# RWKV-7 chains in a hybrid block: small passes moved from VectorE to ScalarE, joint reciprocal roots, and the substitution's rows spread by a transfer to DRAM and back

## The chip, the cores and the metric

The kernel runs on one core of one Trainium2 chip. The metric is the device time of an execution in microseconds (us); less is better. Engines are named as in the profile: PE is TensorE (PEld its weight loads), DVE is VectorE, ACT is ScalarE, POOL is GpSimd, SP is SyncE. SP, ACT and POOL can issue DMA transfers; all transfers share 16 DMA engines.

## The reference

One layer of an encoder block over 256 tokens of width 2048, all in float32. The input is normed and projected; the columns feed an RWKV-7 time mixer (16 heads of 64), a latent attention (8 heads) and two gates. The gated sum is projected and normed back in, then come a gated MLP with a causal convolution, and an embedding branch. The change touches only the RWKV-7 mixer:

```python
def step(state, inp):
    r_t, w_t, k_t, v_t, kk_t, a_t = inp
    sa = jnp.einsum('bhvk,bhk->bhv', state, -kk_t)
    state = (state * w_t[:, :, None, :]
             + sa[..., None] * (kk_t * a_t)[:, :, None, :]
             + v_t[..., None] * k_t[:, :, None, :])
    y_t = jnp.einsum('bhvk,bhk->bhv', state, r_t)
    return state, y_t
...
kk = heads(k * k_k)
kk = kk / jnp.maximum(jnp.sqrt(jnp.sum(kk * kk, axis=-1, keepdims=True)), 1e-12)
k = k * (1 + (a - 1) * k_a)
y = rwkv7_scan(r_h, heads(decay), k_h, v_h, kk, a_h)
mean = jnp.mean(y, axis=-1, keepdims=True)
var = jnp.mean(jnp.square(y - mean), axis=-1, keepdims=True)
y = ((y - mean) * lax.rsqrt(var + RW_GN_EPS)).reshape(B, S, RW_WIDTH)
```

## The kernel before

**The work in the large.** PE runs dense matmuls for nearly the whole span. Each weight chunk (128 x 1024 float32, 512 KB) is loaded by SP into one of three `raw` buffers; ACT casts each half to float32r (`hi`, line 148, five buffers) and DVE subtracts to get the rest (`lo`, line 149, five buffers). Three products (hi x hi, hi x lo, lo x hi; lines 183 to 185) give nearly float32 accuracy. A `raw` buffer is free again when its two `lo` are made, a `hi` or `lo` buffer when PE has used it.

**The RWKV chains.** Between some 187 and 590 us the eight pairs of heads run through `rw_pair`, woven into the dense matmuls of the projections, the attention branch and the gates. A pair is two heads on 128 partitions; two pairs (`par` 0 and 1) run in step as a duo; the four duos are called duo 0 to duo 3. A pair goes through these stages, each a few steps of the generator:

- Preparation: decay, key norm (`pq`, the root in `nv`), the key factor (line 792), the scaled keys and receptances `bk` and `kr`.
- `pg` (line 818): all Gram blocks on PE; DVE masks them (`gm`, line 821), ACT copies the strictly lower part (`n`, 823).
- Substitution: each 64 x 64 unit triangular block is inverted from its 16 x 16 diagonal blocks up. DVE gathers these blocks of both pairs (`dg`, 842) and subtracts them from the identity (848: the diagonal step). Then every partition of a group of 16 needs all 15 rows of its group: 15 stream shuffles (line 854) copy row i of each group to its 16 partitions in `rp16`. Then come 15 columns, each a product `pd` (861) and a reduction into `xc` (862), each dependent on the one before. Both pairs are done in these operations at once.
- The blocks are joined on PE: transposes `Y` (888), then `ph`, `px`, `ph`, `px` (line 882) with DVE between.
- Four chunks of 64 tokens in sequence, three steps each: `pc` (940), the copy `R` of two halves (941 on ACT, 942 on DVE), `pc` again (944), `av` of two halves (945 ACT, 946 DVE), `pc` (953), the state `sv` (955, DVE), which the next chunk's matmul (940) needs.
- Tail: output `yc` (964), group norm of `y` (970 to 982), `pm` (988, transpose-like matmuls of the normed `y`), gate, `yrw`.

**What sets the order.** `rw_pair` is a generator; each `yield` gives a number of dense units (one unit is six matmuls of 256 columns) that are put into the program before the next step: STEP is 2.4, CHUNK 2.8, SUB 1.56. The loop at the end of the stage advances the tail of the old duo, the current one, and the preparation of the next, in that order. What a step emits is then placed on each engine by the framework's list scheduler. Every engine takes its instructions strictly in program order, so an instruction that waits holds up all behind it on its engine.

## Time and profile before

| | |
|---|---|
| median of 3 runs | 1561.18 us (1561.16 to 1561.9) |
| the profiled execution | 1560.39 us, of which the span of its instructions is 1558.6 us |
| PE busy | 1538.0 us, 99% |
| DVE busy | 1182.2 us, 76% |
| ACT busy | 942.1 us, 60% |
| POOL busy | 60.9 us, 4% |
| granted PE clock | 0.997 |

How to read it: in a list of groups each row gives line, engine, operation, output<-inputs, shapes and count, then busy us and the mean ns of one, then the idle time of the engine before them and what ended it. In the list of waits stand the total, the number and the longest. In a row of windows stand the stretch, its length, then busy us and instructions of PE, PEld, DVE, ACT and POOL, the granted clock, the DMA share and GB/s. A timeline row starts with start and duration; the brackets hold the idle time before it. A row of DMA issues gives the size and the median us from issue to landing. Matmuls overlap, so the mean ns of one is longer than its share of the time.

### The profile page before, as it was taken

The page shows a single profiled execution, that of the slowest core. Times are in us where ns is not written, and L with a number is a line of the kernel's source. Part 1 is how long each engine was busy: PE and PEld are TensorE (multiplying, and loading weights), DVE is VectorE, ACT ScalarE, POOL GpSimd, SP SyncE. Part 2 cuts the span into 40 slices and gives each one's busy share as a digit, 9 for nine tenths or more (in the row PEclk, how much of TensorE's full clock was granted, in tenths as well). Part 3 has the DMA queues.
Part 4 walks back from the last instruction along what each step waited for, and adds up shares of the span by engine and source line. Part 5 has one row for each costly group of instructions (what it writes and reads, how often), then busy time and mean ns, then how long its engine had stood idle before and what let it go on. Part 6 is the DMA issues. An engine that isn't in the chain of part 4 may idle for free.

```text
span 1558.6 us, 29636 instructions
## 1 busy us (share of the span) xinstructions
PE 1538.0 (99%) x10850; PEld 1388.3 (89%) x10850; DVE 1182.2 (76%) x2670; ACT 942.1 (60%) x1944; POOL 60.9 (4%) x125
## 2 busy tenths in 40 slices
PE   9999999999999999999999999999999999999997
PEld 9989999999999999887888888888888888888886
DVE  7896687898989776557787777777777655777866
ACT  7686756566565555456766555555655555776653
POOL 0000201101011102000000000000000000000000
PEclk9999999999999999999999999999999999999998
DMA  8654555454444546865656555565655666666564
GB/s 304 192 172 141 154 173 164 138 171 129 147 150 136 160 153 200 306 199 167 203 174 205 198 181 202 179 203 179 206 181 190 175 192 195 197 197 191 166 200 148
DMA packets 80482, 285.19 MB, mean 183 GB/s; under 512 B 9040, under 2 KB 10320, under 8 KB 80336
## 3 DMA queue, kind: packets, MB, share of 16 engines
q1 hardware_dynamic: 77760, 279.48, 56.3%
q10 hardware_dynamic: 2576, 3.81, 0.7%
q8 instruction: 85, 1.39, 0.4%
q14 instruction: 61, 0.50, 0.1%
HBM read 281.16 MB, written 2.10 MB: 182 GB/s over the span
## 4 chain that ended last, share of the span: by engine, by line
PE 89%; DVE 6%; ACT 2%; DMA 1%; issue 1%; DVEq 0%; ACTq 0%
PE d L170 21%; PE d L174 11%; PE d L183 9%; PE d L185 8%; PE d L184 8%; PE o L196 7%; PE o L198 6%; PE o L200 6%; PE e L196 2%; PE e L198 2%; PE e L200 2%; DVE lo L149 2%; ACT hi L148 1%; DMA raw<-in_w_in 1%; PE tr L237 0%
## 5 line engine op out<-in xcount | busy, mean ns | idle before, releaser
L149 DVE TENSOR_TENSOR lo<-raw,hi 128x512 fp32r<-128x512 f32 x684 | 461.0, 690 | 213.9 <-ACT hi L148 208.5
L148 ACT CAST hi<-raw 128x512 fp32r<-128x512 f32 x684 | 410.7, 619 | 297.9 <-PE o L200 97.9
L183 PE MATMUL d<-uT,hi 128*128 128x256 f32 x1072 | 307.7, 287 | 0.7 <-ACT hi L161 0.6
L170 PE MATMUL d<-u,highs 128*128 128x512 f32 x1312 | 305.5, 390 | 0.0
L185 PE MATMUL d<-uT,lo 128*128 128x256 f32 x1072 | 300.5, 280 | 0.7 <-DVE lo L162 0.2
L184 PE MATMUL d<-uT,hi 128*128 128x256 f32 x1072 | 299.6, 279 | 0.1
L170 PEld LDWEIGHTS d<-u,highs 128*128 128x128 f32 x1312 | 243.3, 188 | 48.9
L148 ACT CAST highs<-raw 128x512 fp32r<-128x512 f32 x328 | 186.8, 616 | 115.0 <-DMA raw<-in_w_up 80.3
L183 PEld LDWEIGHTS d<-uT,hi 128*128 128x128 f32 x1072 | 201.7, 188 | 2.8 <-ACT hi L161 0.8
L185 PEld LDWEIGHTS d<-uT,lo 128*128 128x128 f32 x1072 | 201.5, 188 | 2.1 <-DVE lo L149 1.1
L184 PEld LDWEIGHTS d<-uT,hi 128*128 128x128 f32 x1072 | 201.7, 188 | 0.4 <-DVE uT L290 0.3
L149 DVE TENSOR_TENSOR hi<-raw,highs 128x512 fp32r<-128x512 f32 x164 | 112.7, 688 | 76.8 <-PE d L174 58.8
L174 PE MATMUL d<-u,lo 128*128 128x256 f32 x752 | 117.7, 280 | 0.0
L149 DVE TENSOR_TENSOR lo<-raw,highs 128x512 fp32r<-128x512 f32 x164 | 112.0, 684 | 0.0
L174 PE MATMUL d<-u,hi 128*128 128x256 f32 x656 | 103.3, 279 | 0.0
L174 PEld LDWEIGHTS d<-u,lo 128*128 128x128 f32 x752 | 101.7, 188 | 0.8
L174 PEld LDWEIGHTS d<-u,hi 128*128 128x128 f32 x656 | 91.5, 188 | 3.5
L198 PE MATMUL o<-lo,fsplit 128*128 128x512 f32 x264 | 88.6, 389 | 0.0
L196 PE MATMUL o<-hi,fsplit 128*128 128x512 f32 x264 | 88.5, 389 | 0.0
L200 PE MATMUL o<-hi,fsplit 128*128 128x512 f32 x264 | 88.4, 389 | 0.0
L1228 ACT ACTIVATE cy<-d 128x512 f32<-128x512 f32 x44 | 26.2, 597 | 67.8 <-PE d L174 67.8
L198 PEld LDWEIGHTS o<-lo,fsplit 128*128 128x128 f32 x264 | 49.6, 188 | 10.7 <-DVE lo L149 0.3
(389 smaller groups left out, 2550.9 us busy)
## 6 DMA issues: line engine op xcount, KB each, us to landing
raw<-in_w_up SPq DMA_DIRECT2D x176, 512.0 KB, 4.3
raw<-in_w_in SPq DMA_DIRECT2D x133, 512.0 KB, 3.6
raw<-in_w_down SPq DMA_DIRECT2D x88, 512.0 KB, 4.3
raw<-in_w_out SPq DMA_DIRECT2D x32, 512.0 KB, 4.4
raw<-in_w_pg SPq DMA_DIRECT2D x32, 512.0 KB, 3.6
raw<-in_w_bm SPq DMA_DIRECT2D x16, 512.0 KB, 3.7
raw<-in_w_br SPq DMA_DIRECT2D x16, 512.0 KB, 3.7
raw<-in_w_kv SPq DMA_DIRECT2D x8, 512.0 KB, 3.6
```

The costliest lines, as they stand in the source:

```text
L148: nc.scalar.copy(hi[:], raw[:, c:c + 512])
L149: tt(out=lo[:], in0=raw[:, c:c + 512], in1=hi[:].bitcast(F32), op=ALU.subtract)
L170: mm(ps[:, c, :], hi(i, col, P), mov[i][2], start=first and x == 0 and i == 0, stop=False)
L174: mm(ps[:, c, 0:T], lo(i, col, P), mov[i][0], start=False, stop=last and x == len(parts) - 1 and i == len(mov) - 1)
L183: mm(ps[:, c, :], hi(i, col, P), mov[i][:, 0:T], start=f, stop=False)
L184: mm(ps[:, c, :], hi(i, col, P), mov[i][:, T:2 * T], start=False, stop=False)
L185: mm(ps[:, c, :], lo(i, col, P), mov[i][:, 0:T], start=False, stop=l)
L196: mm(b[:], h, hi(i, g * 512, 512), start=f, stop=False)
L198: mm(b[:], h, lo(i, g * 512, 512), start=False, stop=False)
L200: mm(b[:], x, hi(i, g * 512, 512), start=False, stop=l)
L1228: act(y[:], ps[:, :, 0:T], AF.Copy)
```

## The change

- The upper halves of `R` and of `av` go from DVE to ACT.
- The key factor `a * k_a + (1 - k_a)` goes from DVE to ACT.
- The group norm: the centring pass is gone. ACT squares `y` with the negated mean as bias, one instruction per chunk (four per pair in place of one), and scales with root and bias, again one per chunk, in place of a DVE pass per pair.
- The reciprocal roots of both pairs (key norm and group norm) are made in one set of operations on 8 columns in place of two on 4, in the second pair's step.
- The 15 shuffles go. ACT issues a write of `dg` (128 x 128 float32, 64 KB) to a DRAM tile, and POOL a read back: 15 rows of 512 bytes to each of 128 partitions, every group of 16 partitions from the same 15 rows (960 KB). It has seven SUB steps from the diagonal step to the first column where there were six, and a column is followed by a step of 1.45 units (COL).

```diff
--- before.py
+++ after.py
@@ -26,7 +26,7 @@
 NH = 8
 DS = float(np.exp(-0.5))
 
-STEP, CHUNK, SUB = 2.4, 2.8, 1.56
+STEP, CHUNK, SUB, COL = 2.4, 2.8, 1.56, 1.45
 
 
 NONE, READY, FREE, HOLD, AHEAD, TAIL = 0, 2, 3, 5, 6, 7
@@ -705,6 +705,7 @@
     Xbs, krs = [[ep.tile([P, NCH, 2, C], F32, name=f"{nm}{i}") for i in range(2)] for nm in ("Xb", "kb")]
     for n in Xbs + krs:
         nc.gpsimd.memset(n[:], 0.0)
+    rows16 = es_e.enter_context(tc.tile_pool(name="dr", bufs=1, space=bass.MemoryType.DRAM)).tile([P, P], F32, name="rows16")
     rp16 = ep.tile([P, 16, 2 * NCH * 16], F32, name="rp16")
     nc.gpsimd.memset(rp16[:, 15, :], 1.0)
 
@@ -767,12 +768,17 @@
         for t in range(2):
             mm(pq[:, 2 * t:2 * t + 2], sq[:, t * P:t * P + P], K("hsel", 0, 2), start=t == 0, stop=t == 1)
         yield NONE, STEP
-        nv = sp.tile([P, 4, 4], F32, name="nv")
-        ts(out=nv[:, 0, :], in0=pq[:, 0:4], scalar1=1e-24, scalar2=None, op0=ALU.max)
-        rsqrt(nv[:, 1, :], nv[:, 0, :], (nv[:, 2, :], nv[:, 3, :]))
+
+        if par == 0:
+            J["nv"] = sp.tile([P, 4, 2, 4], F32, name="nv")
+        nv = J["nv"]
+        ts(out=nv[:, 0, par, :], in0=pq[:, 0:4], scalar1=1e-24, scalar2=None, op0=ALU.max)
+        if par == 1:
+            nvs = [nv[:, i].rearrange("p r n -> p (r n)") for i in range(4)]
+            rsqrt(nvs[1], nvs[0], nvs[2:])
         yield NONE, STEP
         rb = e1("rb", [P, 4, C])
-        act(rb[:], nv[:, 1, :].unsqueeze(2).to_broadcast([P, 4, C]), AF.Copy)
+        act(rb[:], nv[:, 1, par, :].unsqueeze(2).to_broadcast([P, 4, C]), AF.Copy)
         yield NONE, STEP
         nr = small("nr")
         for t in range(2):
@@ -789,7 +795,7 @@
         be = e1("be")
         tt(out=be[:], in0=kk[:], in1=a[:], op=ALU.mult)
         tt(out=bk[:, :, 0:C], in0=c4(be[:]), in1=c4(pin[:]), op=ALU.mult)
-        ts(out=a[:], in0=a[:], scalar1=V("k_a", j), scalar2=oka[:, j:j + 1], op0=ALU.mult, op1=ALU.add)
+        act(a[:], a[:], AF.Identity, scale=V("k_a", j), bias=oka[:, j:j + 1])
         yield NONE, STEP
         kp = e1("kp")
         tt(out=kp[:], in0=k, in1=a[:], op=ALU.mult)
@@ -847,12 +853,12 @@
             act(x8, i16, AF.Copy)
             tt(out=d8, in0=i16, in1=d8, op=ALU.subtract)
         yield NONE, SUB
-
-        for o in range(0, 15, 3):
-            if par == 1:
-                for i in range(o, o + 3):
-                    nc.vector.stream_shuffle(out=rp16[:, i, :], in_=dg[:].rearrange("p r c j -> p (r c j)"),
-                                             mask=[i] * 16 + [16 + i] * 16)
+        if par == 1:
+
+            nc.scalar.dma_start(rows16[:], dg[:].rearrange("p r c j -> p (r c j)"))
+            nc.gpsimd.dma_start(rp16[:, 0:15, :].rearrange("p i n -> p (i n)"),
+                                bass.AP(rows16.tensor, rows16.offset, [[16 * P, 8], [0, 16], [1, 15 * P]]))
+        for _ in range(6):
             yield NONE, SUB
         for t in range(1, 16):
             if par == 1:
@@ -860,7 +866,7 @@
                 r8 = rp16[:].rearrange("p i (q j) -> p q i j", j=16)
                 tt(out=pd[:, :, 0:t + 1], in0=x8[:, :, 0:t + 1], in1=r8[:, :, 0:t + 1, t], op=ALU.mult)
                 nc.vector.tensor_reduce(out=x8[:, :, t], in_=pd[:, :, 0:t + 1], axis=AX.X, op=ALU.add)
-            yield NONE, SUB
+            yield NONE, COL
         lgs = ep.tile([P, 3, P], F32R, name="lgs", bufs=2)
         act(lgs[:, 0:2, :], lwr[:, 2:4, :], AF.Copy)
         tt(out=lgs[:, 2, :], in0=lwr[:, 2, :], in1=lgs[:, 0, :].bitcast(F32), op=ALU.subtract)
@@ -939,11 +945,11 @@
             o = lambda i, h, hs: pc[hs, i * P + h * C:i * P + h * C + C]
             mm(b(0), two(gm[:, c, 0]), two(sv[:, c]), start=True, stop=True)
             act(R[lo_, :], o(0, 0, lo_), AF.Copy)
-            nc.vector.tensor_copy(R[hi_, :], o(0, 1, hi_))
+            act(R[hi_, :], o(0, 1, hi_), AF.Copy)
             yield NONE, CHUNK
             mm(pc[:, P:P + C], two(Xb[:, c]), R[:], start=True, stop=True)
             act(av[lo_, c, 0, :], o(1, 0, lo_), AF.Copy, scale=-1.0)
-            ts(out=av[hi_, c, 1, :], in0=o(1, 0, hi_), scalar1=-1.0, scalar2=None, op0=ALU.mult)
+            act(av[hi_, c, 1, :], o(1, 0, hi_), AF.Copy, scale=-1.0)
             if c < NCH - 1:
                 pC = pp[:, c, C:C + 1]
                 s0 = ep.tile([P, 2, C], F32, name=f"s0{par}", bufs=1)
@@ -965,21 +971,27 @@
         act(y[:], cc(py), AF.Copy)
         yield TAIL, STEP
 
-        gs = sp.tile([P, 5, NCH], F32, name="gs")
+        if par == 0:
+            J["gs"] = sp.tile([P, 5, 2, NCH], F32, name="gs")
+        gs = J["gs"][:, :, par]
         bc4 = lambda ap: ap.unsqueeze(2).to_broadcast([P, NCH, C])
         nc.vector.tensor_reduce(out=gs[:, 0, :], in_=y[:], axis=AX.X, op=ALU.add)
-        ts(out=gs[:, 0, :], in0=gs[:, 0, :], scalar1=1.0 / C, scalar2=None, op0=ALU.mult)
-        tt(out=y[:], in0=y[:], in1=bc4(gs[:, 0, :]), op=ALU.subtract)
+        ts(out=gs[:, 0, :], in0=gs[:, 0, :], scalar1=-1.0 / C, scalar2=None, op0=ALU.mult)
         yield NONE, STEP
         sq = e1("sq1", [P, NCH, C])
-        act(sq[:], y[:], AF.Square)
+        for c in range(NCH):
+            act(sq[:, c, :], y[:, c, :], AF.Square, bias=gs[:, 0, c:c + 1])
         nc.vector.tensor_reduce(out=gs[:, 1, :], in_=sq[:], axis=AX.X, op=ALU.add)
         ts(out=gs[:, 1, :], in0=gs[:, 1, :], scalar1=1.0 / C, scalar2=64e-5, op0=ALU.mult, op1=ALU.add)
         yield NONE, STEP
-        rsqrt(gs[:, 2, :], gs[:, 1, :], (gs[:, 3, :], gs[:, 4, :]))
+        if par == 1:
+            g8 = [J["gs"][:, i].rearrange("p r n -> p (r n)") for i in range(5)]
+            rsqrt(g8[2], g8[1], g8[3:])
+            tt(out=g8[0], in0=g8[0], in1=g8[2], op=ALU.mult)
         for _ in range(3):
             yield NONE, STEP
-        tt(out=y[:], in0=y[:], in1=bc4(gs[:, 2, :]), op=ALU.mult)
+        for c in range(NCH):
+            act(y[:, c, :], y[:, c, :], AF.Identity, scale=gs[:, 2, c:c + 1], bias=gs[:, 0, c:c + 1])
         yield NONE, STEP
         yield NONE, STEP
         pm = small("pm")
```

How it moves instructions, at three places. Line numbers after the change are up to 12 higher than before it; `x` is the count.

DVE in the third chunk of duo 1, while duo 2 is prepared, up to the state update `sv` (`bk`, `kp`, `a`, `rk` belong to duo 2). Before:

```order
L792 TENSOR_SCALAR a<-a,vec,oka 128x256
L795 TENSOR_TENSOR kp<-z_3277,a 128x256
L149 TENSOR_TENSOR lo<-raw,hi 128x512
L946 TENSOR_SCALAR av<-pc 64x64 x2
L796 TENSOR_TENSOR bk_5740<-kp,pin 128x4x64
L795 TENSOR_TENSOR kp<-z_3277,a 128x256
L149 TENSOR_TENSOR lo<-raw,hi 128x512
L796 TENSOR_TENSOR bk_5744<-kp,pin 128x4x64
L800 SCALAR_TENSOR_TENSOR rk<-z_3452,vec,kp 128x256
L149 TENSOR_TENSOR lo<-raw,hi 128x512
L955 SCALAR_TENSOR_TENSOR sv<-pc,pp_3889,s_5779 64x64 x2
L955 SCALAR_TENSOR_TENSOR sv<-pc,pp_3894,s_5784 64x64 x2
```

After (the key products are lines 801 and 802, `sv` is 961):

```order
L802 TENSOR_TENSOR bk_5688<-kp,pin 128x4x64
L149 TENSOR_TENSOR lo<-raw,hi 128x512
L1025 SCALAR_TENSOR_TENSOR mix<-g,mix 128x512
L801 TENSOR_TENSOR kp<-z_3260,a 128x256
L149 TENSOR_TENSOR lo<-raw,hi 128x512
L802 TENSOR_TENSOR bk_5692<-kp,pin 128x4x64
L806 SCALAR_TENSOR_TENSOR rk<-z_3429,vec,kp 128x256 x2
L149 TENSOR_TENSOR lo<-raw,hi 128x512 x2
L961 SCALAR_TENSOR_TENSOR sv<-pc,pp_3869,s_5727 64x64 x2
L149 TENSOR_TENSOR lo<-raw,hi 128x512
L961 SCALAR_TENSOR_TENSOR sv<-pc,pp_3874,s_5732 64x64 x2
```

The key factor (792) and the halves of `av` (946) are no longer ahead of `sv`, nor are the copies of `R` (942) that stood two rows higher; the second pair's `sv` has a `lo` between it and the first's.

DVE ahead of the first column of duo 1's substitution (`pd` is the product, `xc` the reduction, `lgs` and `yf` belong to the gate and the tail of other pairs). Before:

```order
L854 STREAM_SHUFFLE rp_2510<-dg 128x128
L999 TENSOR_TENSOR yf<-yf,pgt 128x256
L362 SCALAR_TENSOR_TENSOR z_4740<-d,vec,z_4740 128x255
L149 TENSOR_TENSOR lo<-raw,hi 128x512
L999 TENSOR_TENSOR yf<-yf,pgt 128x256
L861 TENSOR_TENSOR pd<-xc,rp_2510 128x8x2
L866 TENSOR_TENSOR lgs<-lwr,lgs 128x128
L862 TENSOR_REDUCE xc<-pd 128x8
L867 TENSOR_TENSOR lgs<-lwr,lgs 32x128
L861 TENSOR_TENSOR pd<-xc,rp_2510 128x8x3
L149 TENSOR_TENSOR lo<-raw,hi 128x512
L862 TENSOR_REDUCE xc<-pd 128x8
```

After (`pd` is line 867):

```order
L1011 TENSOR_TENSOR yf<-yf,pgt 128x256
L362 SCALAR_TENSOR_TENSOR z_4704<-d,vec,z_4704 128x255
L149 TENSOR_TENSOR lo<-raw,hi 128x512
L1011 TENSOR_TENSOR yf<-yf,pgt 128x256
L872 TENSOR_TENSOR lgs<-lwr,lgs 128x128
L873 TENSOR_TENSOR lgs<-lwr,lgs 32x128
L872 TENSOR_TENSOR lgs<-lwr,lgs 128x128
L149 TENSOR_TENSOR lo<-raw,hi 128x512
L873 TENSOR_TENSOR lgs<-lwr,lgs 32x128
L867 TENSOR_TENSOR pd<-xc,rp_2513 128x8x2
L868 TENSOR_REDUCE xc<-pd 128x8
L149 TENSOR_TENSOR lo<-raw,hi 128x512
```

The shuffles are gone; the four `lgs` subtractions stand ahead of the first `pd`, which now waits for the transfer into `rp`. Between the diagonal step and this `pd` there are six `lo` where there were four.

ACT in duo 1, from the last copy of `n` on (`yf` reads `pm`, the matmuls of the normed `y`). Before:

```order
L148 CAST hi<-raw 128x512
L823 ACTIVATE n_4524<-gm_4523 64x256
L824 ACTIVATE gm_4523<-kr_4256 64x4x64
L148 CAST hi<-raw 128x512 x3
L990 ACTIVATE yf<-pm,vec 128x256 x2
L148 CAST hi<-raw 128x512
L361 ACTIVATE z_4740<-d,omu 128x256
```

After (`n` is line 829, the scaling of `y` 994, the write to DRAM 858):

```order
L829 ACTIVATE n_4497<-gm_4496 64x256
L148 CAST hi<-raw 128x512
L830 ACTIVATE gm_4496<-kr_4226 64x4x64
L994 ACTIVATE y<-y,gs 128x64 x2
L148 CAST hi<-raw 128x512
L994 ACTIVATE y<-y,gs 128x64 x2
L148 CAST hi<-raw 128x512
L994 ACTIVATE y<-y,gs 128x64 x3
L148 CAST hi<-raw 128x512
L994 ACTIVATE y<-y,gs 128x64
L858 DMA rows_2512<-dg 128x128
L1002 ACTIVATE yf<-pm,vec 128x256 x2
```

Eight scaling passes and three casts stand between the last `n` and the issue of the write, and ahead of `yf`. On POOL the read back stands after the copies of `kb` and `bk` and ahead of those of `Xb`. PE's matmuls are the same; some chain groups stand six dense matmuls earlier or later.

## The prediction

> **What bounds the kernel now.** I read the page first, then the waits of TensorE (PE) in the stretch that the change touches (187 to 600 us, the RWKV chains), then what the other engines do in it.
>
> ```profile
> PE 1538.0 (99%) x10850; PEld 1388.3 (89%) x10850; DVE 1182.2 (76%) x2670; ACT 942.1 (60%) x1944; POOL 60.9 (4%) x125
> ```
> ```profile
> L184 PE MATMUL d<-uT,hi 128*128 128x256 f32 x1072 | 299.6, 279 | 0.1
> ```
> ```profile
> 0.00:40.00 40.00, 37.70 (x296) 36.57 (x297) 30.49 (x70) 30.22 (x57) 1.43 (x8) 1.00 0.88 306
> 40.00:80.00 40.00, 40.00 (x345) 40.00 (x344) 32.65 (x97) 27.67 (x56) 0.00 (x0) 1.00 0.60 183
> ```
> ```profile
> PE pc L940 <- DVE sv L955: 1.9, 4, 0.9
> PE px L882 <- DVE YH L893: 1.7, 4, 0.6
> PE pc L944 <- DVE R L942: 0.3, 1, 0.3
> PE pb L918 <- DVE Xb L910: 0.2, 1, 0.2
> ```
> TensorE is busy 99% of the span, and the change leaves every matmul in place. So it can win only what TensorE waits for in the chains: 1.9 + 1.7 + 0.3 + 0.2 = 4.1 us in ten waits. Each costs a little more, because matmuls overlap: from 40 to 80 us they start 40/345 = 0.116 us apart and last 0.28, so a restart loses up to 0.16 us. Ten times 0.16 on 4.1 gives a **ceiling of 5.7 us**, 0.37% of the span. Below 0.2% (3.1 us) a measurement of this kernel can't tell a change from none.
>
> All ten waits are for DVE. The largest shows why:
>
> ```profile
> 385.55 1.20 DVE L955 SCALAR_TENSOR_TENSOR sv<-pc,pp,s 64x64 f32<-64x64 f32 x4
> 386.27 0.46 PE L940 MATMUL pc<-sv,gm 128*128 128x128 f32 x2 [0.90 <-DVE sv L955]
> ```
> The state update (L955) started late behind the next duo's rows on DVE. DVE's load from the first column of the substitution to the Y transposes, in the first two duos:
>
> ```profile
> 233.10:249.90 16.80, 16.80 (x146) 16.80 (x145) 16.08 (x50) 7.48 (x15) 0.00 (x0) 1.00 0.55 162
> 325.10:342.10 17.00, 17.00 (x144) 16.72 (x143) 16.31 (x56) 8.18 (x17) 0.00 (x0) 1.00 0.64 187
> ```
> The fourth number is DVE: 16.31 of 17.00 us. The substitution runs at DVE's limit, yet TensorE (the second number) is busy throughout, since it has dense matmuls to run until ph.
>
> **The change part by part.** *Off DVE* (groups by line, 190 to 595 us, here and below; the page's count is of the whole span):
>
> ```profile
> L854 DVE STREAM_SHUFFLE rp<-dg 128x128 f32<-128x128 f32 x60 | 14.4, 298 | 0.0
> L942 DVE COPY R<-pc 64x64 f32<-64x64 f32 x32 | 6.1, 225 | 0.6
> L946 DVE TENSOR_SCALAR av<-pc 64x64 f32<-64x64 f32 x32 | 6.0, 225 | 0.8 <-ACT av L945 0.3
> L792 DVE TENSOR_SCALAR a<-a,vec,oka 128x256 f32<-128x256 f32 x8 | 3.3, 407 | 0.0
> L972 DVE TENSOR_TENSOR y<-y,gs 128x256 f32<-128x256 f32 x8 | 3.4, 424 | 0.2
> L982 DVE TENSOR_TENSOR y<-y,gs 128x256 f32<-128x256 f32 x8 | 3.3, 420 | 0.1
> L222 DVE SCALAR_TENSOR_TENSOR gs<-gs 128x4 f32<-128x4 f32 x8 | 1.3, 158 | 0.0
> ```
> The first six make 36.5 us. Joint roots halve 18 groups like the last one, 9 in each of two roots: 18 x 1.3 / 2 = 12, less four added products of 0.16, so 11. Together some 47 us, 12 per duo. Per chunk, two R copies and two av halves (4 x 0.225) leave, and once per pair L792 (0.41): about 1.3 us ahead of the state update that was 0.9 us late. So I take 1.7 of the 1.9 us, and the 0.3 of R, as won; with 5 x 0.16 of overlap that is **-2.8 us**. The px and pb waits stay: DVE still reaches them from a full stretch.
>
> *Onto ACT:*
>
> ```profile
> L941 ACT ACTIVATE R<-pc 64x64 f32<-64x64 f32 x32 | 6.0, 212 | 4.0 <-PE pc L940 3.9
> L950 ACT ACTIVATE s<-sv,pp 128x128 f32<-128x128 f32 x24 | 9.3, 402 | 5.8 <-DVE sv L955 5.6
> L990 ACT ACTIVATE yf<-pm,vec 128x256 f32<-128x256 f32 x8 | 4.2, 561 | 0.3 <-PE pm L988 0.3
> L975 ACT ACTIVATE sq<-y 128x256 f32<-128x256 f32 x8 | 3.2, 413 | 0.7 <-DVE y L972 0.6
> ACT hi L148 <- PE d L184: 71.0, 96, 1.8
> L148 ACT CAST hi<-raw 128x512 fp32r<-128x512 f32 x227 | 137.5, 617 | 104.0 <-PE d L184 71.0 <-DMA raw<-in_w_in 15.7 <-DVE pd L861 3.3
> ```
> The 64 new halves cost 0.21 each as L941 does (13.4 us). The 128x64 passes with a column for bias or scale are not in the trace; between 0.21 (L941) and 0.56 (L990, four times as wide), near L950's kind at half its width, I take 0.35 for the scaling and 0.30 for the squares: 32 x 0.65 - 3.2 = 17.6. The key factor, L990's form: 8 x 0.56 = 4.5. Sum 35 us. The cover is the 71 us in which ACT waits for TensorE to free a hi buffer; those waits also mean that all five hi buffers, of 12 matmuls or 1.4 us each, are full ahead of TensorE. Within a chunk R is two ops a pair now, 0.85 us for both pairs, and TensorE leaves a step of 2.8 x 6 x 0.117 = 2.0 us for it; with one cast of 0.62 between it fits.
>
> Where it does not fit is the norm of duo 1 (the order shows it):
>
> ```profile
> 314.87 0.41 ACT L823 ACTIVATE n<-gm 64x256 f32<-64x256 f32 x1
> 316.98 1.15 PE L988 MATMUL pm<-cst,y 64*64 64x64 f32 x32
> 312.09 0.75 DVE L982 TENSOR_TENSOR y<-y,gs 128x256 f32<-128x256 f32 x2
> ```
> DVE finished y at 312.8, 4 us before pm. Now eight ACT passes stand behind the last n, with one gm copy and three casts among them: 315.3 + 0.4 + 8 x 0.35 + 3 x 0.6 = 320.3, about 1 us earlier since DVE's part ahead is shorter: 319.3. The second pair's pm is due at 317.5. TensorE waits **1.8 us**; 0.7 at 0.21 a pass, 3.5 at 0.56. In the later duos the passes stand among the n copies, and I count nothing.
>
> *The transfer.* First column after the change: diagonal step, ACT's issue, write to DRAM, POOL's issue, read back 960 KB. Rows:
>
> ```profile
> out<-h ACTq DMA_DIRECT2D x4, 256.0 KB, 2.2
> lwr<-in_w_lora ACTq DMA_DIRECT2D x8, 256.0 KB, 3.0
> raw<-in_w_in SPq DMA_DIRECT2D x133, 512.0 KB, 3.6
> gbc<-in_g_pm SPq DMA_DIRECT2D x2, 512.0 KB, 5.3
> L797 POOL COPY bk<-bk 64x256 f32<-64x256 f32 x8 | 6.7, 840 | 70.1 <-DVE bk L791 70.1
> 227.26 0.29 DVE L848 TENSOR_TENSOR dg<-cst,dg 128x128 f32<-128x128 f32 x1
> 252.56 0.75 PE L882 MATMUL ph<-YH,n 32*32 32x32 f32 x64
> L149 DVE TENSOR_TENSOR lo<-raw,hi 128x512 fp32r<-128x512 f32 x226 | 154.9, 691 | 52.5 <-ACT hi L148 48.0 <-PE d L184 2.6 <-PE yc L964 1.0
> L362 DVE SCALAR_TENSOR_TENSOR z<-d,vec,z 128x255 f32<-128x255 f32 x16 | 7.6, 474 | 0.0
> 317.10 0.28 DVE L848 TENSOR_TENSOR dg<-cst,dg 128x128 f32<-128x128 f32 x1
> 341.55 0.50 DVE L888 STREAM_TRANSPOSE YH<-Xc 128x128 f32<-128x128 f32 x2
> 342.85 0.75 PE L882 MATMUL ph<-YH,n 32*32 32x32 f32 x64
> ```
> Write: 2.2 as out (no less, 3.0 as lwr at most). Read: the first 40 us moved 306 GB/s (last number of the first window above), which makes 3.2 us of 960 KB, and raw shows 3.6 - 1.7 = 1.9 around it: 5.1 at least; 9.9 if it goes as gbc, a load that repeats one row for all partitions; I take 6, nearer raw, since gbc stands behind a raw in its queue. POOL issues no DMA in the trace: its copies take twice ACT's, so 0.7 (0.4 to 1.0). ACT's issue stands behind the eight passes in duo 1: 2.0 us; in the others 0.3 to 1. Together 10.9 us in duo 1, 9.2 to 9.9 elsewhere; bounds 7.8 and 15.9.
>
> The cover: in duo 1 the columns to Y took 325.1 to 342.05, 16.9 us; less some 0.8, as the four small lgs subtractions now run ahead, 16.1. Ph at 342.85 wants the first column by 326.6: 9.2 us after the diagonal step ends at 317.4. Late by 1.7, but pm has held TensorE back 1.8 by then, so nothing is added there; in duo 0 the columns took 16.8, of which two splits (0.69 each) and two z mixes (0.47) move ahead: 14.5, and ph at 252.56 wants the first column by 238.0, 10.5 after the step ends at 227.55. I take duos 2 and 3 as between the two: even. Queued behind the waiting pd on DVE are lo splits, which hi's lead covers for some 4 us; behind ACT's issue, casts; behind POOL's, only Xb copies due after ph. I add **0.3 us**. The shorter column step (COL for SUB) pays for the two added steps: 7 x 1.56 + 15 x 1.45 = 32.7 units against 21 x 1.56 = 32.8, so ph does not move.
>
> The Trainium skill, "DMA: Bandwidth & Descriptors", anatomy of a gpsimd DMA, gives 2.0 us plus a ns for every 436 bytes: an estimate of 4.3 us for this read, by which the transfer is in time in every duo and the sum 0.3 us lower. For raw's 512 KB it gives 3.2 where the trace has 3.6; no run here shows a read from POOL.
>
> Sum: -2.8 + 1.8 + 0.3 = **-0.7 us** on the profiled execution's 1560.39; on the median, 1561.18, which is 0.8 above it: **1560.5**.
>
> **The rivals.**
> 1. *Faster.* The passes cost 0.25, or pm finds y ready; then px and pb waits ease as well, as DVE starts the columns with no arrears. -2.8 to -5.5: 1555.7 to 1558.4. For it: DVE loses 47 us where every wait is DVE's. Against: px comes right after the fullest stretch.
> 2. *Slower by the transfer.* One place, the first pd, in order on DVE. It decides from a round trip of 10 us; each further us stops TensorE one us in four duos. At 12 us: 4 x 2 - 2.8, +5 (1566); at the bound of 15.9 it is +20. For it: 960 KB beside weights that keep the DMA engines half busy (0.55 and 0.64 in the windows above), from an engine that issues none now. Against: the rows of half the size. The skill's "SBUF — State Buffer" warns that DVE blocks such a DMA's descriptors in its two-port modes, though it leaves tensor_tensor out, and that is what runs there.
> 3. *Slower by ACT.* All four norms late as in duo 1, at 0.5 a pass: 4 x 2.5 - 2.8 = +7 (1568). For it: ACT's rows at the n copies are dense. Against: four us of slack before.
>
> **How the numbers follow.** Forecast (within 0.2% either way) 0.40; rival 1 0.36, of which a tenth stays under 0.2%; rival 2 0.16; rival 3 0.08. So faster 0.34, same 0.41, slower 0.25. The range, 1556 to 1568, takes rival 1 to its end and rivals 2 and 3 to their middle.
>
> **What would show it.** The L854 groups gone and DVE some 47 us less busy, ACT 35 more. PE's waits on sv and R gone, a wait of pm on ACT's y of 1 to 2 us near 317. The DMA row of rp with its landing: under 7 us after issue. First pd 9 to 11 us after the diagonal step. Wrong if ph or lo L149 heads TensorE's waits (rival 2), if pm waits in every duo (rival 3), or if no wait is left (rival 1).

## The result and the profile after

The changed kernel takes **1594.79 us** (median of 5 runs, 1592.39 to 1597.99) against 1561.18 us before (5 runs, 1560.69 to 1562.54): ratio **1.0216**, 95% interval 1.0204 to 1.0229 (below, such a ratio to the kernel before and its interval stand in brackets). It is 33.6 us slower; forecast were 1560.5 us and a range that ended at 1568. The profiled execution after took 1595.25 us with a span of 1593.5.

Busy time of the engines in the kernel after:

```profile
PE 1549.9 (97%) x10850; PEld 1397.8 (88%) x10850; DVE 1148.3 (72%) x2394; ACT 978.2 (61%) x2072; POOL 61.7 (4%) x129
```

DVE lost 34 us and ACT gained 36, so the work moved as planned; TensorE fell from 99% to 97% of a longer span. Its waits in the kernel after (total us, times, longest):

```profile
PE d L185 <- DVE lo L149: 22.0, 6, 6.9
...
PE px L888 <- DVE YH L899: 1.3, 3, 0.6
PE pm L1000 <- ACT y L994: 1.3, 3, 0.5
...
PE pc L946 <- DVE sv L961: 1.0, 3, 0.5
```

Before, the largest of these sums was 1.9 us, on sv. Now the dense matmuls wait 22 us for `lo`, a weight split that is no part of the chains. DVE's waits and DVE's timeline around one of them show what stands ahead of it:

```profile
DVE pd L867 <- DMA rp<-rows: 37.0, 4, 11.2
```
```profile
337.03 0.28 DVE L873 TENSOR_TENSOR lgs<-lwr,lgs 32x128 fp32r<-32x128 f32 x1
344.31 0.18 DVE L867 TENSOR_TENSOR pd<-xc,rp 128x16 f32<-128x16 f32 x1 [6.99 <-DMA rp<-rows]
344.53 0.17 DVE L868 TENSOR_REDUCE xc<-pd 128x8 f32<-128x16 f32 x1
344.61 0.69 DVE L149 TENSOR_TENSOR lo<-raw,hi 128x512 fp32r<-128x512 f32 x1
```

The first column `pd` waits 7 us for the read, and the split comes right behind it on DVE. The transfers, by issue (KB of one, median us to landing):

```profile
rp<-rows POOLq DMA_DIRECT2D x4, 960.0 KB, 13.8
...
lwr<-in_w_lora ACTq DMA_DIRECT2D x8, 256.0 KB, 4.1
...
rows<-dg ACTq DMA_DIRECT2D x4, 64.0 KB, 2.2
```

The write lands in 2.2 us by the median (1.5 to 4.3), as forecast; the read takes 13.8. Per duo, from the trace (us of the span):

| | duo 0 | duo 1 | duo 2 | duo 3 |
|---|---|---|---|---|
| diagonal step ends | 228.9 | 327.2 | 424.4 | 523.4 |
| write lands | 231.8 | 328.8 | 428.7 | 524.9 |
| read issued | 232.1 | 329.4 | 429.2 | 525.5 |
| read lands | 246.5 | 344.3 | 440.4 | 538.6 |
| issue to landing of the read | 14.4 | 14.9 | 11.2 | 13.2 |
| first column after the diagonal step | 17.6 | 17.1 | 16.1 | 15.3 |

Nor is the read alone late. The stretch of the second read in the kernel after (us of PE, PEld, DVE, ACT, POOL, then clock, share of the DMA engines, GB/s):

```profile
329.40:344.30 14.90, 12.83 (x112) 12.29 (x112) 6.12 (x14) 5.91 (x13) 0.54 (x1) 1.00 0.88 178
```

The DMA engines are busy 0.88 of the time and move 178 GB/s; before, the same kind of stretch moved 187 GB/s at 0.64. A weight load issued at 330.9 landed after 13.9 us, one at 335.4 after 11.3, where loads away from the reads have a median of 3.6. So three things may be to blame: the read's own form, the column that holds up DVE, the weights that come late; and the passes on ACT may add to it.

A fourth loss stands in no list of waits. TensorE's longest stand (time in which it runs nothing) is 6.9 us in duo 0, 2.6 in duo 1, 6.4 in duo 2 and 5.5 in duo 3. Here is the one in duo 3, the work right behind it, and an equal stretch after that (columns as above):

```profile
534.00:539.50 5.50, 0.05 (x1) 0.00 (x0) 0.83 (x3) 0.59 (x2) 0.00 (x0) 0.94 0.35 99
539.50:545.70 6.20, 6.19 (x29) 6.20 (x30) 5.80 (x21) 2.80 (x6) 0.00 (x0) 0.50 0.53 168
545.70:551.90 6.20, 6.20 (x54) 6.20 (x54) 5.86 (x19) 2.49 (x4) 0.00 (x0) 1.00 0.52 161
```

The granted clock is 0.50 for 6.2 us of work, and 29 matmuls run where 54 run in the same time later; the dense ones start 0.21 us apart in place of 0.12. The same is seen for 4.3 us behind the stand of duo 0 and 4.4 us behind that of duo 2, and not behind the 2.6 us of duo 1. Together 14.9 us of TensorE's work ran at half clock; by the two spacings that cost some 7 us (an estimate). In the kernel before, the clock is 1.00 all through the chains; over the whole execution it is 0.997 before and 0.991 after, and 0.988 to 0.991 in all five executions after.

### The profile page after: what moved, and what is told of

Its sections match the earlier page's. It is cut to its first block, busy times and chain, and to the rows that moved or that the text cites. A ratio compares the mean times of both kernels' runs of the same rounds, so it can differ in the third digit from the quotient of the medians.

```text
span 1593.5 us, 29536 instructions
## 1 busy us (share of the span) xinstructions
PE 1549.9 (97%) x10850; PEld 1397.8 (88%) x10850; DVE 1148.3 (72%) x2394; ACT 978.2 (61%) x2072; POOL 61.7 (4%) x129
## 4 chain that ended last, share of the span: by engine, by line
PE 84%; DMA 6%; DVE 5%; ACT 3%; issue 1%; DVEq 0%; SPq 0%; ACTq 0%; POOLq 0%
PE d L170 20%; PE d L174 10%; PE d L183 8%; PE d L185 8%; PE d L184 8%; PE o L198 6%; PE o L200 6%; PE o L196 6%; DMA rp<-rows 3%; PE e L196 2%; PE e L198 2%; PE e L200 2%; DVE lo L149 2%; ACT hi L148 1%; DMA raw<-in_w_in 1%
## 5 line engine op out<-in xcount | busy, mean ns | idle before, releaser
L185 PE MATMUL d<-uT,lo 128*128 128x256 f32 x1072 | 304.6, 284 | 21.4 <-DVE lo L149 21.4
L183 PE MATMUL d<-uT,hi 128*128 128x256 f32 x1072 | 312.0, 291 | 0.5 <-ACT hi L161 0.5
L184 PE MATMUL d<-uT,hi 128*128 128x256 f32 x1072 | 303.4, 283 | 0.0
L185 PEld LDWEIGHTS d<-uT,lo 128*128 128x128 f32 x1072 | 205.6, 192 | 22.5 <-DVE lo L149 22.2
L183 PEld LDWEIGHTS d<-uT,hi 128*128 128x128 f32 x1072 | 206.0, 192 | 2.5 <-ACT hi L161 0.8
L184 PEld LDWEIGHTS d<-uT,hi 128*128 128x128 f32 x1072 | 205.9, 192 | 0.1
L198 PEld LDWEIGHTS o<-lo,fsplit 128*128 128x128 f32 x264 | 49.6, 188 | 10.6 <-DVE lo L149 0.3
```

The lines of the kernel that those rows point to most:

```text
L183: mm(ps[:, c, :], hi(i, col, P), mov[i][:, 0:T], start=f, stop=False)
L184: mm(ps[:, c, :], hi(i, col, P), mov[i][:, T:2 * T], start=False, stop=False)
L185: mm(ps[:, c, :], lo(i, col, P), mov[i][:, 0:T], start=False, stop=l)
L198: mm(b[:], h, lo(i, g * 512, 512), start=False, stop=False)
```

## The experiments

**One half each.** First the transfer alone undone, then the transfer alone put into the kernel before.

```diff
-            nc.scalar.dma_start(rows16[:], dg[:].rearrange("p r c j -> p (r c j)"))
-            nc.gpsimd.dma_start(rp16[:, 0:15, :].rearrange("p i n -> p (i n)"),
...
+                for i in range(o, o + 3):
+                    nc.vector.stream_shuffle(out=rp16[:, i, :], in_=dg[:].rearrange("p r c j -> p (r c j)"),
```

> The changed kernel with the transfer alone undone: the 15 shuffles stand on VectorE again and the step counts are the old ones; the moves to ScalarE and the joint roots stay. Theory (the transfer is the whole loss): the 33.6 us of loss are gone and the rest keeps its gain of up to some 3 us: 1558 to 1561.5 us, and rp leaves TensorE's chain. Rival (the norm passes and halves on ScalarE cost time of their own): 1564 us or more, with pm or pc heading TensorE's waits.

Measured: 1565.26 us against 1560.98 (1.0027, 1.0018 to 1.0037): the rival holds.

> The kernel before with the transfer alone: write, read back and the step counts of the change; every pass stays on VectorE as before. Theory (the transfer is the whole loss): 1592 to 1600 us, the read lands 11 to 15 us after its issue, and lo of line 149 heads TensorE's waits. Rival (the transfer is slow only beside the fuller ScalarE, or the loss is shared): under 1585 us.

Measured: 1598.27 us (1.0237, 1.0222 to 1.0252), lo waited for 27.8 us, the reads landed after 12.4 to 14.5 us: the theory's figures hold. Taken out of the change, the transfer is worth 29.5 of the 33.6 us (1594.8 - 1565.3); put into the kernel before, it costs 37.3, more than the whole change. So the parts don't add up to one price. The profiled spans of the changed kernel and of the run with the shuffles are 29.3 us apart; 21 of these are time in which TensorE stood longer (43.6 us not busy against 22.3), and the estimated 7 us of half clock are nearly all of the rest. Without the transfer, the rest of the change is no gain either: it loses 4.3 us. Where these are is shown by the groups by line, 160 to 660 us, of the kernel before and then of the run with the shuffles (busy us, mean ns of one, idle before and its releaser):

```profile
L988 PE MATMUL pm<-cst,y 64*64 64x64 f32 x128 | 4.6, 221 | 0.0
```
```profile
L993 ACT ACTIVATE y<-y,gs 128x64 f32<-128x64 f32 x32 | 12.4, 432 | 2.6 <-DVE gs L989 2.5
L999 PE MATMUL pm<-cst,y 64*64 64x64 f32 x128 | 7.2, 231 | 1.8 <-ACT y L993 1.8
```

The 128 pm matmuls take 7.2 us and 1.8 of wait where they took 4.6 and none. From start to start it is 8.6 against 4.3 us: each quarter of them waits for ACT's pass over its own chunk, and the passes come 0.34 us apart with casts in between. The list of waits shows just 1.8 of this, since a matmul that runs alone counts as busy. The timelines say why the passes come late, here at the first of the four norms (same run, ACT and then DVE):

```profile
311.98 0.42 ACT L828 ACTIVATE n<-gm 64x256 f32<-64x256 f32 x1 [1.97 <-DVE gm L826]
...
315.75 0.42 ACT L829 ACTIVATE gm<-kr 64x256 f32<-64x256 f32 x1
316.19 0.77 ACT L993 ACTIVATE y<-y,gs 128x64 f32<-128x64 f32 x2
```
```profile
313.62 0.16 DVE L222 SCALAR_TENSOR_TENSOR gs<-gs 128x8 f32<-128x8 f32 x1
313.70 0.69 DVE L826 TENSOR_TENSOR gm<-pg,cst 128x512 f32<-128x512 f32 x1
314.30 0.16 DVE L989 TENSOR_TENSOR gs<-gs 128x8 f32<-128x8 f32 x1
```

The joint root is one chain of dependent small operations in which the gm operations take turns; it ends at 314.5. Before, the two pairs' roots ran between each other, a step about every 0.1 us, and ended at 311.6. Then ACT has the copies of n ahead in order until 316.2.

**The norm apart.** Group norm as before on top of the run with the shuffles:

```diff
+        tt(out=y[:], in0=y[:], in1=bc4(gs[:, 0, :]), op=ALU.subtract)
-            act(sq[:, c, :], y[:, c, :], AF.Square, bias=gs[:, 0, c:c + 1])
+        act(sq[:], y[:], AF.Square)
-            act(y[:, c, :], y[:, c, :], AF.Identity, scale=gs[:, 2, c:c + 1], bias=gs[:, 0, c:c + 1])
+        tt(out=y[:], in0=y[:], in1=bc4(gs[:, 2, :]), op=ALU.mult)
```

> The kernel with the shuffles and with the group norm's passes as before (centring and scaling on VectorE, one square on ScalarE); of the change stay the halves of R and av and the key factor on ScalarE, and the joint roots. Theory (in the run with the shuffles, the 128 pm matmuls took 8.6 us from start to start where they took 4.3 before, since each pair of them waits for the ScalarE pass of its own chunk, and that is the whole 4.3 us that the run lost): 1558 to 1561 us, not slower than before, and pm takes 4.3 us again. Rival (the halves, the key factor or the roots cost time as well): 1562 us or more with pm at 4.3.

Measured: 1560.57 us against 1561.47 (0.9995, 0.9986 to 1.0004), pm at 4.3 us: the theory holds. The loss of 4.3 us is the norm's passes; what is left of the change can't be told from before.

Instead, on the run with the shuffles, the passes two steps earlier in the code:

```diff
-        for _ in range(3):
-            yield NONE, STEP
+        yield NONE, STEP
         for c in range(NCH):
             act(y[:, c, :], y[:, c, :], AF.Identity, scale=gs[:, 2, c:c + 1], bias=gs[:, 0, c:c + 1])
+        for _ in range(2):
+            yield NONE, STEP
```

> The run with the shuffles (all moves to ScalarE and the joint roots, no transfer), with the scaling passes of the norm put one step after the root in place of three, two steps earlier; pm stays where it was. Theory (pm was slow because the passes came too late, not because ScalarE has too much): pm takes 4.3 to 5 us from start to start in place of 8.6, and 1559 to 1562 us. Rival (ScalarE is too full: casts now stand behind the passes): 1564 us or more, with hi of line 148 or pm in TensorE's waits.

Measured: 1565.69 us (1.0024, 1.0014 to 1.0035), pm at 8.7 us. The time is the rival's, but its reason isn't seen: the first pass starts at 315.9, behind the same copies of n (311.6 to 315.8), so that nothing has moved on ACT. The place in the code is not what held them.

**Halves of R and av alone**, in the kernel before:

```diff
-            nc.vector.tensor_copy(R[hi_, :], o(0, 1, hi_))
+            act(R[hi_, :], o(0, 1, hi_), AF.Copy)
-            ts(out=av[hi_, c, 1, :], in0=o(1, 0, hi_), scalar1=-1.0, scalar2=None, op0=ALU.mult)
+            act(av[hi_, c, 1, :], o(1, 0, hi_), AF.Copy, scale=-1.0)
```

> The kernel before with one part of the change alone: the upper halves of R and av on ScalarE. Prediction's term: 2.8 us won, 1557.5 to 1559.5. Rival (the waits on sv are set by VectorE's rows of the next duo, and the two halves now follow one another on ScalarE): within 0.2% of before, and sv still waited for by about 1.3 us.

Measured: 1560.75 us against 1561.3 (0.9995, 0.9986 to 1.0003). TensorE's waits:

```profile
PE px L882 <- DVE YH L893: 2.0, 4, 0.6
...
PE pc L940 <- DVE sv L955: 0.9, 4, 0.4
```

R's wait is gone, sv's is 0.9 in place of 1.9, px's is 0.3 up. By the interval the effect lies between -2.2 and +0.5 us, so the term of -2.8 was too large. (That term also counted the key factor; the run with the norm's passes back has it moved too, and lies between -2.2 and +0.6.)

**The form of the read.** Six runs changed the source, the count or the queue, each from the changed kernel:

```diff
-                                bass.AP(rows16.tensor, rows16.offset, [[16 * P, 8], [0, 16], [1, 15 * P]]))
...
+            for u, w in ((0, 8), (8, 15)):
...
+                                    bass.AP(rows16.tensor, rows16.offset + u * P, [[16 * P, 8], [0, 16], [1, (w - u) * P]]))
...
+                                bass.AP(rows16.tensor, rows16.offset, [[16 * P, 16], [0, 8], [1, 15 * P]]))
...
+                                bass.AP(rows16.tensor, rows16.offset, [[15 * P, P], [1, 15 * P]]))
...
+                                bass.AP(rows16.tensor, rows16.offset, [[16 * 15 * P + P, 8], [15 * P, 16], [1, 15 * P]]))
...
+                                bass.AP(rows16.tensor, rows16.offset, [[8 * 15 * P + P, 16], [15 * P, 8], [1, 15 * P]]))
...
-            nc.gpsimd.dma_start(rp16[:, 0:15, :].rearrange("p i n -> p (i n)"),
+            nc.scalar.dma_start(rp16[:, 0:15, :].rearrange("p i n -> p (i n)"),
```

> The changed kernel with the read back cut into two transfers from POOL, rows 0 to 7 and rows 8 to 14 of every group, 512 and 448 KB, each with the same outer count of 8. Theory A (one such transfer runs on 8 of the 16 DMA engines, since its source has 8 groups as its outermost count; two run on 16): packets stay near 300 ns of wait-free time, the data stretch falls from 8.6 to 12.9 us to 5 to 7, the last of the two lands 8 to 10 us after the first issue, and the time falls by 4 x 4 to 5 us to 1572 to 1580. Theory B (16 readers of the same DRAM rows in a group wait for each other) and theory C (the weight stream takes the share): the last lands 11 to 15 us after the first issue as before, 1590 to 1600. The Trainium skill, "DMA: Bandwidth & Descriptors", how many engines (k), gives such an access pattern k = 8, as theory A has it.

> The changed kernel with the rows written twice (a second write of 64 KB on ScalarE's queue, so that each group of 16 partitions has two copies of its rows), and read with an outermost count of 16, 8 partitions to a copy. Theory A (8 of 16 DMA engines): the read lands 7 to 9 us after its issue in place of 11 to 15, 1566 to 1578 us. Theory B (several readers of the same rows): every row still has 8 readers, so it lands at 10 us or later, 1586 to 1598. Theory C (the weight stream): no change, 1590 to 1600.

> The changed kernel, but the read back takes 128 different rows of 7680 bytes from a DRAM tile that was filled from a weight (so the substitution gets wrong rows; the write of dg still comes first and is waited for): no source row is read twice, and the outermost count is 128. Theory A (8 of 16 engines is the whole slowness): it lands 7 to 9 us after its issue, as the read with an outermost count of 16 did at best. Theory B (readers of the same rows also hold each other up): packets take near 300 ns in place of 480 to 570, and it lands 5 to 6.5 us after its issue. Theory C (the share of the weights): 10 us or more.

> As the run with 128 different rows, but with the source's outermost count at 8 (8 groups of 16 different rows, a gap of 512 bytes between the groups; the substitution gets wrong rows here too). Theory A: at most some 9 or 10 packets under way at a time as in the changed kernel, and a landing of 10 to 15 us although no row is read twice. Theory B: packets near 300 ns, landing at 7 to 9 us. If it lands as the run with the outermost count of 128, the count has nothing to do with it.

> As the run with 128 different rows, but the source counted as 16 groups of 8 different rows (a gap of 512 bytes between the groups; the substitution gets wrong rows). All 128 rows differ, and the destination is the same. Theory D (what makes a packet slow is the form: an engine that writes a run of neighbouring partitions; the outermost count alone decides): packets of 480 to 570 ns as in the run with two copies of the rows, landing 7.3 to 11.4 us. Theory B (several readers of one row): packets of some 300 to 340 ns and a landing of 7.2 to 9 us as in the run with the outermost count of 128.

> The changed kernel with the read issued by ScalarE's queue in place of POOL's; the same source and destination. ScalarE waits in order for the write, so casts stand behind it for 2 to 4 us; only the landing is to be read. Theory A (8 engines): 10 us or more from issue to landing here too, data stretch 8 to 12 us. Rival (POOL makes the descriptors too slowly): landing at 5 to 8 us.

In the order of the added lines above: two reads, rows written twice, the three with 128 different rows, ScalarE's queue. Measured, from the traces (packets of the read; the stretch is from the first packet's start to the last one's end). The times of the three with 128 different rows and of ScalarE's queue are from one execution each, the others medians of four or five; - stands where the trace has no landing:

| source's outermost count | readers of a row | most packets at once | packet, mean ns | stretch, us | issue to landing, us | slowest weight load beside it, us | time, us |
|---|---|---|---|---|---|---|---|
| 8 (the change) | 16 | 9 to 10 | 462 to 650 | 8.6 to 12.4 | 11.2 to 14.9 | 13.9 | 1594.8 |
| 8 | 1 | 10 to 11 | 420 to 626 | 8.1 to 11.8 | 10.8 to 15.0 | 11.8 | 1594.5 |
| 16 | 8 | 17 to 21 | 484 to 574 | 5.3 to 8.3 | 7.3 to 11.3 | 10.4 | 1585.3 |
| 16 | 1 | 18 to 19 | 501 to 523 | 5.9 to 8.0 | 8.4 to 10.2 | 9.0 | 1581.6 |
| 128 | 1 | 17 to 19 | 296 to 338 | 4.7 to 7.0 | 7.2 to 9.0 | 8.1 | 1575.3 |
| two reads of 8 | 16 | 19 to 20 | 366 to 459 (4096 bytes), 645 to 804 (7168 bytes) | 6.9 to 9.5 | 10.5 to 13.3, first issue to last landing | 10.1 | 1594.8 |
| 8, ScalarE's queue | 16 | 10 | 563 to 602 | 10.3 to 12.1 | - | - | 1594.3 |

The issue rows of the second, third and fifth of them:

```profile
rp<-rows POOLq DMA_DIRECT2D x4, 960.0 KB, 13.0
```
```profile
rp<-rows POOLq DMA_DIRECT2D x4, 960.0 KB, 8.9
```
```profile
rp<-rows POOLq DMA_DIRECT2D x4, 960.0 KB, 8.2
```

The outermost count decides: with 8, at most some 10 packets are under way, with 16 or more some 18, and the landing falls from 13 to 9 us. Whether 16 partitions or one read a row makes no difference to the landing (first against second line, third against fourth), and with 128 came theory B's short packets but not its landing of 5 to 6.5 us: theory B is out. The issuing queue makes none either. Theory A and theory D, by which the count alone decides, hold for the packets and the landings of single reads, but for the rows written twice theory A was too good: it had 7 to 9 us and 1566 to 1578, measured 7.3 to 11.3 and 1585.3. And it fails for the two reads of half the size: with as many packets under way as with 16 they gained little, where it expected 8 to 10 us for the last landing. Their packets of 7168 bytes took longer than those of 7680 in the single read; why is open. Nor is a packet's own duration the measure: with 128 it falls by a third, and the landing by 0.8 us.

The Trainium skill, "DMA: Bandwidth & Descriptors", rules for kernel authors, has just this: an outermost count under 16 confines a DMA to at most that many engines. The packets under way agree (10 against 18); the traces name no engines.

**More cover.** Thirteen steps in place of seven between the diagonal step and the first column:

```diff
-        for _ in range(6):
+        for _ in range(12):
             yield NONE, SUB
```

> The changed kernel with 13 steps of 1.56 units in place of 7 between the diagonal step and the first column (some 6.6 us more cover in each duo), nothing else. Theory (each us by which the read is later than its cover stops TensorE one us, in four duos, and the rest of the loss is pm's 4 us): 1566 to 1572 us, and rp and lo of line 149 leave TensorE's waits. Rival (the read's traffic slows the weights, or the time of the chains themselves decides): 1580 us or more.

Measured: 1603.87 us (1.0271, 1.0257 to 1.0285), lo waited for 21.5 us, the first column 15.7 to 18.4 us after the diagonal step. The expectation failed, first of all since the edit didn't add the cover that it was to add: in DVE's order 6, 4, 5 and 5 lo splits stood between the diagonal step and the first column, against 6, 6, 5 and 4 with seven steps. So more steps didn't put more work ahead of the column; that the scheduler places the column by the landing that it reckons with fits this, but isn't shown. Nor are the 9 us that the run lost on the changed kernel a matter of cover: TensorE stood only 0.8 us longer (44.4 against 43.6), but it worked 29.2 us at half clock against 14.9, some 6.5 us by the spacings above, and pm took 10.6 us against 7.3. So the columns' start copy was made from a small matmul at that place, which TensorE reaches in order:

```diff
-            act(x8, i16, AF.Copy)
+            mm(px8[:, 0:16], ident, K("i16", 0, 16), start=True, stop=True)
+            act(x8, px8[:, 0:16].unsqueeze(1).to_broadcast([P, 2 * NCH, 16]), AF.Copy)
```

> The changed kernel with 13 steps ahead of the first column and the columns' start copy taken from a matmul of the identity at that place (16 columns, one per duo), so that the columns can't be put earlier in VectorE's order: 10 or 11 lo splits stand between the diagonal step and the first column in place of 4 to 6. Theory (what the late read costs is the splits that stand behind the waiting column): TensorE's wait for lo of line 149, 22 us in the changed kernel, falls under 4 us, and the time is 25 us under the run with 13 steps and no gate, 1575 to 1582 us, the rest being pm and the longer chain. Rival (the read slows the weights themselves): 1590 us or more with lo or hi still heading the waits.

> The run with the shuffles (no transfer) with the same 13 steps and the same gate: what the longer chain costs without any transfer. If the longer chain is free (dense matmuls fill it), 1565 us as without them; if it costs, as much above 1565 as the run with the gate is above it. Theory: 1565 to 1575, within 4 us of the run with the gate and the transfer. Rival (the transfer costs beyond its lateness): over 8 us under that run.

Measured: with the gate and the transfer 1597.39 us (1.0232, 1.0217 to 1.0247), with the gate and shuffles 1565.33 (1.0025, 1.0015 to 1.0034). The longer chain costs nothing, and 10 or 11 splits stood ahead of the column; still the transfer costs 32 us. The rival holds. TensorE's waits, then ACT's (200 to 600 us), of the run with the gate and the transfer:

```profile
PE d L183 <- ACT hi L148: 15.1, 5, 7.4
...
PE d L185 <- DVE lo L149: 2.1, 6, 0.9
```
```profile
ACT hi L148 <- DMA raw<-in_w_in: 35.1, 14, 6.0
ACT lws L734 <- DMA lwr<-in_w_lora: 22.4, 4, 10.8
```

The wait for lo is nearly gone, and a wait for hi, whose casts wait for weights, has taken its place. The second of ACT's rows belongs to it: ACT stood up to 10.8 us for a small weight load of its own (`lwr`, 256 KB, as late as the others), with casts behind it in its order; TensorE's longest wait, 7.4 us, comes right behind that one. ACT with the gate and the shuffles:

```profile
ACT hi L148 <- DMA raw<-in_w_in: 4.5, 4, 1.5
```

Loads issued from 334.7 to 351.4 us, with the transfer and then with the shuffles:

```profile
raw<-in_w_in SPq DMA_DIRECT2D x2, 512.0 KB, 12.6
rp<-rows POOLq DMA_DIRECT2D x1, 960.0 KB, 16.6
raw<-in_w_bm SPq DMA_DIRECT2D x1, 512.0 KB, 10.7
lwr<-in_w_lora ACTq DMA_DIRECT2D x2, 256.0 KB, 14.9
```
```profile
raw<-in_w_in SPq DMA_DIRECT2D x6, 512.0 KB, 3.8
```

Three weight loads in place of six were issued, and they took three times as long. So the late loads stop TensorE by themselves. The column does so too: in duo 2 of the changed kernel the weight loads beside the read landed after 5.0 us at most, and still TensorE stood 6.4 us, since DVE waited at `pd` for 10.3 us and ACT for 11.3 us for the `lgs` subtraction behind it. Each holdup hides the other; what each costs in the changed kernel as a whole these runs don't separate.

**All mended at once.** The gate with the norm's passes back, and then with the count of 16 too:

> The run with the gate, and the group norm's passes as before (centring and scaling on VectorE). Theory: pm back at 4.3 us from start to start, 4 to 8 us under the run with the gate alone. Rival (pm was late because the chain was): no difference.

Measured: 1586.78 us (1.0165, 1.0152 to 1.0179), 10.6 under the run with the gate, with pm back at 4.3 us. The norm weighs more there than the 4.3 us it has without a transfer. In the traces pm took 10.0 us with the gate and ScalarE's passes, 5.7 more; and TensorE's work at half clock falls from 18.2 to 10.4 us, some 3.5 us by the spacings above.

> The run with the gate and the group norm's passes as before, with the rows written twice and read with an outermost count of 16. Theory (on half of the engines the read holds up every weight load beside it, since each of these is spread over all of them): the read lands 7 to 10 us after its issue in place of 15 to 16, weight loads beside it at 5 to 8 us in place of up to 14, TensorE's wait for hi of line 148 falls from 13.6 us to under 4, 1562 to 1570 us. Rival (960 KB are too much beside the weights whatever the form): 1575 us or more, with hi still over 8 us. Not faster than before by either.

Measured: 1574.21 us (1.0076, 1.0059 to 1.0093).

```profile
PE d L183 <- ACT hi L148: 8.1, 3, 3.6
```

The wait for hi fell from 13.6 to 8.1 us, and the read landed 7.1 to 11.5 us after its issue. That lies between theory and rival, and nearer the rival: even with the count of 16 the run is 13.6 us above the same kernel with shuffles and no gate (1560.57). The half clock is a part of what is left: in the four executions the granted clock went from 0.993 to 0.998, and the time from 1577.3 to 1571.6.

**Half the bytes.** On the run with the norm's passes back, rows 0 to 7 by shuffles, and rows 8 to 14 by a transfer that isn't needed until column 8:

```diff
+            nc.scalar.dma_start(rows16[:], dg[:].rearrange("p r c j -> p (r c j)"))
+            nc.gpsimd.dma_start(rp16[:, 8:15, :].rearrange("p i n -> p (i n)"),
+                                bass.AP(rows16.tensor, rows16.offset + 8 * P, [[16 * P, 8], [0, 16], [1, 7 * P]]))
-        for o in range(0, 15, 3):
+        for o in (0, 2, 4, 6, 8):
```

> On the run with the group norm's passes back: rows 0 to 7 spread by eight shuffles, rows 8 to 14 by a transfer of 448 KB, which the column 7 or 8 waits for, some 15 us after the diagonal step; the step counts of the kernel before. Theory (the price of the transfer is only its lateness): the transfer lands 12 to 14 us after the diagonal step, no wait at the columns, VectorE 8 us less busy: 1558 to 1561 us, the same as before or a little under it. Rival (the transfer costs by its share of the DMA engines too, or lands later): 1563 us or more, with lo or ph heading TensorE's waits.

Measured: 1562.94 us against 1561.59 (1.0005, 0.9997 to 1.0014): no difference. The read landed after 5.5 to 7.8 us, the slowest load beside it after 6.9, and lo was waited for 1.7 us. The time is nearer the rival's, but the wait that the rival expected isn't there, nor any gain from the eased DVE. No version beat the kernel before.

## Why the prediction was wrong

- **The read, the step that failed.** "I take 6, nearer raw", bounds 5.1 and 9.9; it took 11.2 to 14.9. Its 3.2 us came from 306 GB/s, which is what the DMA engines moved at a share of 0.88 in the first 40 us, while the windows beside it had them at 0.55 and 0.64 with 162 and 187 GB/s. From those same rows an estimate was to be had: full use is 162/0.55 = 295 and 187/0.64 = 292 GB/s; the weights leave some 118; 0.983 MB at 118 GB/s is 8.3 us without loss to the weights, and twice that, 16.7, if only half of the engines serve it. Measured data stretches of a single read were 4.7 to 8.8 us with counts of 16 and 128, and 8.1 to 14.4 with 8 (the longest with the gate): the estimate, made afterwards, lies at the upper end of the first and above the second. The form of the read, its outermost count, had no term at all in the prediction. The estimate of 4.3 us by the Trainium skill, "DMA: Bandwidth & Descriptors", anatomy of a gpsimd DMA, goes by the bytes alone; the fastest of these reads took 7.1.
- **The rest of the round trip.** Its lower bound adds up to 8.0 us, not 7.8. ACT's issue, 2.0 us in duo 1, came 0.03 us after the diagonal step in every duo. The write's 2.2 us is its median; duo 2's 4.3 is over the bound of 3.0.
- **The cover.** 9.2 and 10.5 us (9.4 for the first by its own terms), and "each further us stops TensorE one us in four duos". The four first columns came 66.1 us after their diagonal steps, 26 over four times 10; TensorE stood 21 us longer than in the run with shuffles, and half clock brought the transfer to 29.5. So rival 2 had the place and the sign that would show it, lo at the head of TensorE's waits, with a bound for the read that was too low; that its price per us comes near the total is in part luck. Its mechanism was half of it: it counted what waits behind the column, and neither what the read takes from the weights, which stops TensorE by itself, nor the slower clock behind a long stand.
- **The ceiling.** That the change could win 5.7 us at most was not contradicted: relief on DVE is worth nothing that can be measured (0.9995 in two runs, and 1.0005 in the one with half the bytes transferred).
- **Off DVE.** Forecast -47 us, measured -34. The groups were right (joint roots 22.8 to 12.5 us, forecast -11), but their sum isn't, since operations of different groups overlap on DVE: the 14.4 us of the shuffles' group were 10.3 of DVE's busy time (1158.6 - 1148.3, without and with the transfer).
- **sv and R.** Forecast -2.8; alone, a ratio of 0.9995, -0.8 us with an interval of -2.2 to +0.5. The wait on R went as said, that on sv halved; px took some of it back.
- **ACT.** +35 forecast, +36 measured; a scaling pass at 0.34 us from start to start (0.35 taken), a square at 0.24 (0.30).
- **pm.** Forecast 1.8 us in one duo and, in the later duos, "I count nothing". Without the transfer it measured 4.3 us over all four: there too pm waits pass by pass. Rival 3 had the mechanism at 2.5 us a duo.
- **The chances.** By the terms given, faster comes to 0.32 and same to 0.44, not 0.34 and 0.41; nothing hangs on it.

## What to carry to other kernels

A transfer beside a stream that sets the pace is priced with what that stream leaves (the bandwidth at full share less what it uses), not with what the DMA engines move without it, and then the other way round: what does the stream lose. Write both sides of a spread or broadcast so that the outermost count is 16 or more, and look in the trace at how many packets are under way and how soon the last one lands. Before more cover is asked for, see in the order whether the steps really put work ahead of the waiting instruction. Look at the granted clock behind every long stand of TensorE: what the stand costs may be more than its length. And a pass cut by chunk paces the matmuls behind it although little of it shows as a wait.

## What was not expected of the hardware

- In the changed kernel the transfer with an outermost count of 8 slowed loads that have nothing to do with it from 3.6 to as much as 13.9 us (10.4 with 16, 8.1 with 128).
- Behind stands of 5.5 to 6.9 us TensorE worked at a granted clock of 0.50 for 4.3 to 6.2 us, its dense matmuls 0.21 us apart in place of 0.12; behind a stand of 2.6 us it did not. The length alone doesn't decide: the run with the halves of R and av alone has 3.4 us at half clock right behind a wait of 1.8 us, at 93 us, and the kernel before has the same wait (1.7 us) without it.
- Packets of the same 7680 bytes took 296 to 338 ns where the source was counted as 128 rows, and 501 to 523 where the same kind of rows was counted as 16 times 8. Why is open; it moved the landing by less than a us, and the time, in one run each, by 6, but with 16 TensorE also stood 6.0 us longer and worked 12.7 us at half clock against 3.4, so that the time doesn't tell what the packets themselves are worth.
- From POOL's issue to the first data packet 1.4 to 2.8 us passed, in the changed kernel and in the runs with 128 different rows.
